# The transform of the long filters: as one full product, and as two half-size products that pass through DRAM

## The chip, the cores and the metric

The kernel runs on one core of one Trainium2 chip. The metric is the time of one execution on the device, in microseconds. A core has a matrix engine (TensorE; the profile calls its matmuls PE and its weight loads PEld), three engines for elementwise work (VectorE = DVE, ScalarE = ACT, GpSimd = POOL) and a queue engine (SyncE = SP). Each engine runs its own list of instructions in order and waits on semaphores for the others. Data reach on-chip memory by DMA; matmuls write into eight banks of PSUM.

## The reference, cut to what matters

One encoder layer on 512 tokens of width 2048. Half of its mixing branch is a Hyena operator: a gated long convolution whose filter is itself computed by a small network (33 to 64 to 64 to 64 to 2048 = 1024 channels forward and 1024 backward).

```python
h = jnp.sin(fr * (z @ w1 + b1))            # three layers of this kind, 64 wide
...
h = h @ w4                                 # last layer: 2 x 1024 channels
h_fwd = h[:, :HYENA_W] * decay
h_bwd = h[:, HYENA_W:] * decay
k = jnp.concatenate([h_fwd, jnp.zeros((1, HYENA_W), f32), h_bwd[:0:-1]], axis=0)
k = k / jnp.sum(jnp.abs(k), axis=0, keepdims=True)
...
z = hv * x1
z = bidir_fft_conv(z, filt) + hy_bias * z  # circular convolution of length 2L = 1024
y_h = z * x0
```

Beside it run grouped-query attention, gates, an output projection and a SwiGLU feed-forward layer; they are not changed.

## The kernel before

All matrices are kept transposed (channels on the 128 rows, 512 tokens along a row). A float32 product is made of three float32r products: each operand is split into a high part (a cast on ScalarE) and a low part (a subtraction on VectorE), and `mm3` issues high x high, high x low and low x high. Weights come as tiles of eight 128x128 blocks: `wblk` (L165 to L167) loads a tile on SyncE's queue (`wr`), casts it on ScalarE (`wh`) and subtracts on VectorE (`wl`), with three tiles of each part alive; 24 matmuls use up one tile.

The main line of the first stage is `group`: 16 blocks of three matmuls for one output tile (`px`, `phv`), for the three projections of each of eight channel tiles. After each block it calls `step()`, which advances a queue of generators by one step; a `yield n` in a generator lets n blocks of the main line pass. So the side work of the Hyena branch is sewn into the projections, and its place in TensorE's list is fixed by these counts (`mm` keeps program order). The other engines' lists are put in order by the scheduler of the build.

The side work is, in this order: `mlp_gen` (the three Sin layers; products `hp`, result `h`), then for each of four slices of 256 channels `filter_gen(q)` and `conv_gen(q)`. `filter_gen` loads `w4`, multiplies it with `h` in float32 (64 rows; products `fp`, L308), multiplies by the decay (`fd`, `bd`, L310), forms sum and difference of the two directions (`hs`, `hd`), transposes them (`ktp`) and splits the four tiles (`ks`). `conv_gen` transposes and splits the data (`ztp`, `zt`), and then for each of four frequency tiles `k` makes the filter's spectrum and the data's spectrum, multiplies them and transforms back:

```python
for j in range(4):
    mm3(kp, Th[j][:, ks], Tl[j][:, ks], ksT[j][0], ksT[j][1], j == 0, j == 3)
K = work(f"K{q}{k}")                       # two ScalarE and two VectorE passes turn kp into K (L372 to L375)
yield 3
up = ps_tile(f"up{q}{k}")                  # 12 matmuls of 256 columns, from zT
...                                        # Y = up * K (L384 to L388), split into Yt
yield 3
if k > 0:
    inverse(k - 1)                         # 12 matmuls of 256 columns into ab
    yield 3
```

`T` are the tables of the 512x512 transform in two parts, loaded once by POOL's queue. `tmp` hands out five rotating scratch tiles, `work` six. At a slice's end `abs` and `y` (L400 to L408) bring the result back to the token order and add the bias term; `y` and `yh` are their tiles.

Of the kernel before, what the change touches and what calls it, by code (L numbers as in the profile page):

```python
# [10 lines left out]
F32 = mybir.dt.float32  # L11
F32R = mybir.dt.float32r
AF = mybir.ActivationFunctionType
ALU = mybir.AluOpType
# [83 lines left out]
    return out  # L98


def layer_kernel(tc, wpk, xT, par, flt, zemb, w4, decT, tbl, rope, qkg, out):
    nc = tc.nc
    PSUM = bass.MemoryType.PSUM

# [44 lines left out]
    def tmp(name):  # L149
        return tpool.tile([P, S], F32, tag="tmp", bufs=5, name=name)  # L150
# [113 lines left out]
    Th, Tl = [], []  # L264

    C1 = 6.28125
    C2 = float(np.float32(2 * math.pi - C1))
# [5 lines left out]
    def mlp_gen():  # L273


        hcur = zem
        yield MLP_WAIT
        for l in range(3):
            nk = 33 if l == 0 else 64
            hp = ps_tile(f"hp{l}")  # L280
            mm(hp[:64], fl[:nk, l * 64:(l + 1) * 64], hcur[:nk], True, True)
            a = tmp(f"ha{l}")[:64]
            nn = tmp(f"hn{l}")[:64]
            nc.vector.tensor_scalar(a, hp[:64], fl[:, 192 + l:193 + l], fl[:, 195:196], ALU.add, ALU.mult)
# [5 lines left out]
            hcur = (tmp(f"h{l}") if l < 2 else cw("h3", [P, S], "h3"))[:64]  # L290
            nc.scalar.activation(hcur, a, AF.Sin)
            yield MLP_WAIT
        mlp["h"] = hcur

    filt = {}

    def filter_gen(q):

        w4s = cw(f"w4{q}", [64, 512], "w4", 1)
        nc.scalar.dma_start(w4s, w4[q])  # L300
        rn, hs_l, hd_l = [], [], []
# [26 lines left out]
        ksT = []  # L328
        for j in range(4):
            tp = ps_tile(f"ktp{q}{j}")  # L330
            for i, src in enumerate((hs_l[0], hs_l[1], hd_l[0], hd_l[1])):
                transpose(tp[:, i * P:(i + 1) * P], src[:, j * P:(j + 1) * P])
            ksT.append(split(cv, tp, "kh", "kl", 4, 4, f"ks{q}{j}"))
            yield 2
        filt[q] = (rn, ksT)

    zst, x0st, yh = {}, {}, [None] * HT

    def conv_gen(q):

        rn, ksT = filt[q]
        while q not in zst or side["n"] < zst[q][2]:
            yield 1
        zl, zf_l, _ = zst[q]
# [20 lines left out]

        for k in range(4):
            ks = slice(k * P, (k + 1) * P)
            kp = ps_tile(f"kp{q}{k}")
            for j in range(4):
                mm3(kp, Th[j][:, ks], Tl[j][:, ks], ksT[j][0], ksT[j][1], j == 0, j == 3)  # L370
            K = work(f"K{q}{k}")
            nc.scalar.activation(K[:, :256], kp[:, :256], AF.Copy, scale=pcol("cosw", k))  # L372
            nc.scalar.activation(K[:, 256:], kp[:, :256], AF.Copy, scale=pcol("nsinw", k))
            nc.vector.scalar_tensor_tensor(K[:, :256], kp[:, 256:], pcol("sinw", k), K[:, :256], ALU.mult, ALU.add)
            nc.vector.scalar_tensor_tensor(K[:, 256:], kp[:, 256:], pcol("cosw", k), K[:, 256:], ALU.mult, ALU.add)  # L375
# [630 lines left out]
def _constants():  # L1006
    f4 = np.float32
    i = np.arange(S)
    t64 = np.cos(np.pi * ((2 * i[:, None] + 1) * (2 * i[None, :] + 1) % 4096) / 2048.0).astype(f4)
    u = t64.view(np.uint32)  # L1010
    hi = (((u.astype(np.uint64) + 0x7FF + ((u >> 12) & 1)) >> 12) << 12).astype(np.uint32).view(f4)
    lo = t64 - hi
    tbl = np.stack([hi, lo]).reshape(2, 4, P, S)
# [17 lines left out]
    for half, pp in ((0, tok // 64), (1, tok % 64)):  # L1031
# [70 lines left out]
```

## Time and profile before

| | |
|---|---|
| median of 3 runs | 2658.74 us (2657.42 to 2659.44) |
| the profiled execution | 2661.56 us |
| its span, first to last instruction | 2659.8 us |
| TensorE busy, share of the span | 99% |
| VectorE, ScalarE, POOL | 61%, 38%, 2% |
| data moved | 293.58 MB, 110 GB/s over the span |
| mean granted TensorE clock | 0.997 of full |

The page's 40 slices show TensorE busy in nine tenths or more of each slice. The filters and the long convolution lie between some 60 and 415 us. The rows on which the prediction rests stand in the section behind the change. In a timeline, a row is the start in us, the duration in us, the engine, the line of the program, the operation, out<-in, and how many instructions of a kind are merged; in brackets is how long the engine was idle ahead of it and who released it. "ACTq" and "POOLq" rows are the issues of DMAs.

### The profile page before, as it was taken

The page shows a single profiled execution, that of the slowest core. Times are in us where ns is not written, and L with a number is a line of the kernel's source. Part 1 is how long each engine was busy: PE and PEld are TensorE (multiplying, and loading weights), DVE is VectorE, ACT ScalarE, POOL GpSimd, SP SyncE. Part 2 cuts the span into 40 slices and gives each one's busy share as a digit, 9 for nine tenths or more (in the row PEclk, how much of TensorE's full clock was granted, in tenths as well). Part 3 has the DMA queues.
Part 4 walks back from the last instruction along what each step waited for, and adds up shares of the span by engine and source line. Part 5 has one row for each costly group of instructions (what it writes and reads, how often), then busy time and mean ns, then how long its engine had stood idle before and what let it go on. Part 6 is the DMA issues. An engine that isn't in the chain of part 4 may idle for free.

```text
span 2659.8 us, 32756 instructions
## 1 busy us (share of the span) xinstructions
PE 2638.1 (99%) x13062; PEld 2219.2 (83%) x13062; DVE 1620.7 (61%) x2285; ACT 1001.2 (38%) x1449; POOL 65.1 (2%) x126
## 2 busy tenths in 40 slices
PE   9999999999999999999999999999999999999999
PEld 7777888788888888888788888888888888788887
DVE  7766654566333333544699898988988862443343
ACT  6333323466222222333454444444444442322111
POOL 0000001110000000000000000000000000000000
PEclk9999999999999999999899999999999999999999
DMA  6222123211223322344333333333333343442343
GB/s 207 78 69 74 60 72 107 80 56 56 96 95 97 101 95 95 123 143 150 99 111 117 121 121 118 127 126 112 121 126 127 118 140 103 153 148 95 123 147 107
DMA packets 90325, 293.58 MB, mean 110 GB/s; under 512 B 10459, under 2 KB 11419, under 8 KB 90172
## 3 DMA queue, kind: packets, MB, share of 16 engines
q1 hardware_dynamic: 71856, 251.69, 29.0%
q10 hardware_dynamic: 12684, 23.02, 2.9%
q0 software_dynamic: 5632, 16.78, 1.6%
q8 instruction: 102, 1.67, 0.3%
q14 instruction: 51, 0.42, 0.0%
HBM read 272.58 MB, written 18.87 MB: 110 GB/s over the span
## 4 chain that ended last, share of the span: by engine, by line
PE 96%; DVE 2%; DMA 1%; ACT 1%; issue 0%; SPq 0%; POOL 0%; ACTq 0%; DVEq 0%; POOLq 0%
PE fx L117 18%; PE d L117 17%; PE g L117 13%; PE fy L117 9%; PE px L117 7%; PE o L117 7%; PE b L117 7%; PE fz L117 5%; PE phv L117 3%; PE q L117 2%; PE kv L117 2%; PE kp L117 2%; PE ab L117 1%; PE up L117 1%; PE av L117 1%; PE sp L117 1%
## 5 line engine op out<-in xcount | busy, mean ns | idle before, releaser
L166 ACT CAST wh<-wr 128x1024 fp32r<-128x1024 f32 (+1 forms) x291 | 304.1, 1046 | 892.7 <-PE d L117 301.0
L167 DVE TENSOR_TENSOR wl<-wr,wh 128x1024 fp32r<-128x1024 f32 (+1 forms) x291 | 352.7, 1212 | 444.8 <-ACT wh L166 442.4
L117 PE MATMUL d<-act,wh 128*128 128x512 f32 x1408 | 435.4, 390 | 2.5 <-DVE act L871 2.0
L117 PEld LDWEIGHTS d<-act,wh 128*128 128x128 f32 x1408 | 264.2, 188 | 60.7 <-DVE act L871 3.9
L781 ACT CAST whs<-s 128x1024 fp32r<-128x1024 f32 x176 | 185.1, 1052 | 244.8 <-PE fx L117 113.1
L117 PE MATMUL d<-act,wl 128*128 128x512 f32 x704 | 273.9, 389 | 0.0
L782 DVE TENSOR_TENSOR wls<-s,whs 128x1024 fp32r<-128x1024 f32 x176 | 214.9, 1221 | 7.6 <-ACT whs L781 2.6
L781 ACT CAST wha<-a 128x1024 fp32r<-128x1024 f32 x132 | 138.9, 1052 | 205.1 <-PE fx L117 97.8
L117 PE MATMUL g<-xh,wh 128*128 128x512 f32 x512 | 200.4, 391 | 0.0
L117 PE MATMUL g<-xl,wh 128*128 128x512 f32 x512 | 199.3, 389 | 0.0
L117 PE MATMUL g<-xh,wl 128*128 128x512 f32 x512 | 199.3, 389 | 0.0
L117 PE MATMUL fx<-X,wha 128*128 128x512 f32 x704 | 179.1, 396 | 5.7 <-DVE c L919 2.9
L117 PE MATMUL fx<-X,whs 128*128 128x512 f32 x704 | 178.1, 395 | 0.4 <-DVE v L797 0.4
L117 PE MATMUL fy<-X,whs 128*128 128x512 f32 x704 | 177.2, 393 | 0.0
L782 DVE TENSOR_TENSOR wla<-a,wha 128x1024 fp32r<-128x1024 f32 x132 | 161.2, 1222 | 8.1 <-ACT wha L781 3.4
L117 PEld LDWEIGHTS d<-act,wl 128*128 128x128 f32 x704 | 132.1, 188 | 27.4
L117 PEld LDWEIGHTS fx<-X,wha 128*128 128x128 f32 x704 | 127.8, 191 | 29.5 <-issue 5.7
L117 PEld LDWEIGHTS fx<-X,whs 128*128 128x128 f32 x704 | 127.6, 190 | 23.9 <-DVE v L797 0.9
L117 PEld LDWEIGHTS fy<-X,whs 128*128 128x128 f32 x704 | 126.8, 189 | 22.7
L117 PEld LDWEIGHTS g<-xh,wl 128*128 128x128 f32 x512 | 96.1, 188 | 20.0
L117 PEld LDWEIGHTS g<-xl,wh 128*128 128x128 f32 x512 | 96.2, 188 | 19.2
L117 PEld LDWEIGHTS g<-xh,wh 128*128 128x128 f32 x512 | 96.2, 188 | 19.1
(1175 smaller groups left out, 4766.8 us busy)
## 6 DMA issues: line engine op xcount, KB each, us to landing
wr<-wpk SPq DMA_DIRECT2D x287, 512.0 KB, 3.3
a<-wpk SPq DMA_DIRECT2D x176, 512.0 KB, 3.8
actd<-c POOLq DMA_DIRECT2D x40, 256.0 KB, 5.0
actr<-actd ACTq DMA_DIRECT2D x40, 256.0 KB, 4.0
xr<-xT SPq DMA_DIRECT2D x16, 256.0 KB, 5.7
x<-xT ACTq DMA_DIRECT2D x16, 256.0 KB, 2.9
x2d<-x POOLq DMA_DIRECT2D x16, 256.0 KB, 3.4
x2r<-x2d ACTq DMA_DIRECT2D x16, 256.0 KB, 2.7
```

Source lines behind the costliest of these rows:

```text
L117: tc.keep_in_program_order(nc.tensor.matmul(out, lhsT=lhsT, rhs=rhs, start=start, stop=stop, **kw))
L166: nc.scalar.copy(hi[:, c], raw[:, c])
L167: nc.vector.tensor_tensor(lo[:, c], raw[:, c], hi[:, c].bitcast(F32), ALU.subtract)
L781: nc.scalar.copy(hi, w)
L782: nc.vector.tensor_tensor(lo, w, hi.bitcast(F32), ALU.subtract)
```

## The change

The filter transform moves from `conv_gen` into `filter_gen` and is done in another way. `hs` and `hd` are stored with their second half reversed, so that rows m and 511-m of the transform meet. After the transposes, each pair of tiles is turned by a position's angle into `u` and `v` (`ku`, `kv`; two ScalarE and two VectorE passes), split, and multiplied by half-size cosine and sine tables `CS` (256 positions by 256 frequencies, loaded by POOL's queue at the start). Sum and difference of the two products (`ke`, `ko`) are the even and the odd frequencies; after the same four passes as before each is written with every second row of a 512x512 DRAM tile `kd[q]`, and `conv_gen` reads it back in frequency order, tile by tile, as `K`. The last layer of the filter network and the one before it change too: the last Sin layer gives its 64 results twice, on 128 rows, and `w4` is held as high part on rows 0 to 63 and low part on rows 64 to 127, so that a product is two float32r matmuls with `hh` and `hl` in place of one float32 matmul.

```diff
-    fl = cw("fl", [64, 196], "fl")
+    fl = cw("fl", [P, 324], "fl")[:, :268]
...
+            nr = 64 if l < 2 else P
-            mm(hp[:64], fl[:nk, l * 64:(l + 1) * 64], hcur[:nk], True, True)
+            mm(hp[:nr], fl[:nk, l * 64:l * 64 + nr], hcur[:nk], True, True)
...
-        mlp["h"] = hcur
+        hh, hl = cw("hh", [P, S], "hh", dt=F32R), cw("hl", [P, S], "hl", dt=F32R)
+        nc.scalar.copy(hh, hcur)
+        nc.vector.tensor_tensor(hl, hcur, hh.bitcast(F32), ALU.subtract)
+        mlp["h"] = hh, hl
...
     def filter_gen(q):
-        w4s = cw(f"w4{q}", [64, 512], "w4", 1)
-        nc.scalar.dma_start(w4s, w4[q])
+        w4r = tmp(f"w4r{q}")
+        w4h = tpool.tile([P, S], F32R, tag="tmp", bufs=5, name=f"w4h{q}")
+        w4s = cw(f"w4s{q}", [P, 512], "w4s", 1, F32R)
+        for h in range(2):
+            nc.scalar.dma_start(w4r[h * 64:(h + 1) * 64], w4[q])
+        nc.scalar.copy(w4h[64:], w4r[64:])
+        nc.scalar.copy(w4s[:64], w4r[:64])
+        nc.vector.tensor_tensor(w4s[64:], w4r[64:], w4h[64:].bitcast(F32), ALU.subtract)
...
-                mm(fp, w4s[:, half * 256 + c * P:half * 256 + (c + 1) * P], mlp["h"], True, True)
+                mm(fp, w4s[:, csl], mlp["h"][0], True, False)
+                mm(fp, w4s[:, csl], mlp["h"][1], False, True)
...
-            nc.vector.tensor_tensor(hs, fd, bd[:, 1:], ALU.add)
-            nc.vector.tensor_tensor(hd[:, ::-1], fd, bd[:, 1:], ALU.subtract)
+            nc.vector.tensor_tensor(hs[:, :256], fd[:, :256], bd[:, 1:257], ALU.add)
+            nc.vector.tensor_tensor(hs[:, :255:-1], fd[:, 256:], bd[:, 257:], ALU.add)
+            nc.vector.tensor_tensor(hd[:, 256:], fd[:, :256], bd[:, 1:257], ALU.subtract)
+            nc.vector.tensor_tensor(hd[:, 255::-1], fd[:, 256:], bd[:, 257:], ALU.subtract)
...
-            ksT.append(split(cv, tp, "kh", "kl", 4, 4, f"ks{q}{j}"))
-            yield 2
+            nc.scalar.activation(u, ab_[0], AF.Copy, scale=fcol("cosb", j))
+            nc.scalar.activation(v, ab_[0], AF.Copy, scale=fcol("nsinb", j))
+            nc.vector.scalar_tensor_tensor(u, ab_[1], fcol("sinb", j), u, ALU.mult, ALU.add)
+            nc.vector.scalar_tensor_tensor(v, ab_[1], fcol("cosb", j), v, ALU.mult, ALU.add)
+            uv.append([split(cv, t, "kh", "kl", 4, 4, f"k{n}{q}{j}") for n, t in (("us", u), ("vs", v))])
+            yield 3
+        yield 6
+        kd[q] = dpool.tile([S, S], F32, tag=f"kd{q}", bufs=1, name=f"kd{q}")
+        for k in range(2):
+            for i in range(2):
+                kp = ps_tile(f"kp{q}{k}{i}")
+                for j in range(2):
+                    sl = slice(j * 256 + k * P, j * 256 + (k + 1) * P)
+                    mm3(kp, CS[i][0][:, sl], CS[i][1][:, sl], uv[j][i][0], uv[j][i][1], j == 0, j == 1)
+                yield 2
+            se = tmp(f"ks{q}{k}")
+            nc.scalar.copy(se, cs[1])
...
+                if i == 0:
+                    nc.gpsimd.dma_start(kd[q][256 * k:256 * k + 255:2], K)
+                elif k == 0:
+                    nc.gpsimd.dma_start(kd[q][1:254:2], K[1:])
+                    nc.gpsimd.dma_start(kd[q][511:512], K[:1])
+                else:
+                    nc.gpsimd.dma_start(kd[q][255:510:2], K)
...
     def conv_gen(q):
         for k in range(4):
-            kp = ps_tile(f"kp{q}{k}")
-            for j in range(4):
-                mm3(kp, Th[j][:, ks], Tl[j][:, ks], ksT[j][0], ksT[j][1], j == 0, j == 3)
             K = work(f"K{q}{k}")
...
-            yield 3
+            nc.gpsimd.dma_start(K, kd[q][ks])
             up = ps_tile(f"up{q}{k}")
...
+    for j in range(2):
+        t = [cw(f"CS{i}{j}", [P, S], f"cs{i}{j}", 1, F32R) for i in range(2)]
+        for i in range(2):
+            nc.gpsimd.dma_start(t[i], tb2[i, j])
+        CS.append(t)
```

The order of instructions changes with it. ScalarE's list around the last Sin layer (`h`), ahead of slice 0's first product, before:

```order
L455 ACTIVATE yh_691<-x00u,prm 128x512
L291 ACTIVATE h_644<-ha_635 64x512
L166 CAST wh_844<-wr_843 128x1024
L315 ACTIVATE scr_766,n_765<-fd_744 128x512
L316 ACTIVATE scr_766,n_765<-bd_745 128x512
L304 DMA dec_777<-decT 128x512
```

and the same place now (`w4r` is the raw tile, `w4s` and `w4h` its parts, `scr` reads the first products' results):

```order
L297 ACTIVATE h_652<-ha_643 128x512
L313 DMA w4r_752<-w 64x512
L519 ACTIVATE yh_699<-x00u,prm 128x512
L301 CAST hh<-h_652 128x512
L313 DMA w4r_752<-w 64x512
L315 CAST w4s_754<-w4r_752 64x512
L166 CAST wh_870<-wr_869 128x1024
L314 CAST w4h_753<-w4r_752 64x512
L333 ACTIVATE scr_786,n_785<-fd_762 128x512
L334 ACTIVATE scr_786,n_785<-bd_763 128x512
```

The load of `w4`, which stood near the start of the program, and its casts now stand between the last Sin and the first passes on the product. VectorE's list at the end of slice 1, ahead of slice 2's first product (`fp`, read by `fd`), before:

```order
L404 SCALAR_TENSOR_TENSOR y_1993<-z_1086,prm,y_1993 128x512
L403 TENSOR_TENSOR y_2000<-abs_1998 128x256
L408 TENSOR_TENSOR yh_1494<-yh_1494,y_1993 128x512
L404 SCALAR_TENSOR_TENSOR y_2000<-z_1380,prm,y_2000 128x512
L310 TENSOR_TENSOR fd_2012<-fp_2014,dec_2010 128x512
L408 TENSOR_TENSOR yh_1650<-yh_1650,y_2000 128x512
```

and now:

```order
L463 SCALAR_TENSOR_TENSOR y_2061<-z_1095,prm,y_2061 128x512
L462 TENSOR_TENSOR y_2068<-abs_2066 128x256
L467 TENSOR_TENSOR yh_1563<-yh_1563,y_2061 128x512
L463 SCALAR_TENSOR_TENSOR y_2068<-z_1427,prm,y_2068 128x512
L316 TENSOR_TENSOR w4s_2078<-w4r_2076,w4h_2077 64x512
L467 TENSOR_TENSOR yh_1695<-yh_1695,y_2068 128x512
L328 TENSOR_TENSOR fd_2086<-fp_2088,dec_2084 128x512
```

The low part of `w4s`, an operand of the product, stands behind the four `y` passes of slice 1. POOL's list behind the loads of the tables `T`, before:

```order
L436 DMA T_415<-tbl 128x512
L436 DMA T_417<-tbl 128x512
L529 TENSOR_TENSOR rpk<-rpk,gaink 128x128 x8
```

and now, the part of slice 0:

```order
L495 DMA T_415<-tbl 128x512
L495 DMA T_417<-tbl 128x512
L395 DMA kd_978<-K_1017 128x512
L397 DMA kd_978<-K_1023 127x512
L398 DMA kd_978<-K_1023 16x1x32
L435 DMA K_1127<-kd_978 128x512
L395 DMA kd_978<-K_1062 128x512
L400 DMA kd_978<-K_1068 128x512
L435 DMA K_1162<-kd_978 128x512
L435 DMA K_1224<-kd_978 128x512
L435 DMA K_1293<-kd_978 128x512
```

Between the tables and the attention's work (`rpk`) now stand nine transfers for each slice; a read waits for the writes of its rows. The four loads of `CS` stand at the very start of POOL's list, the first ahead of the second step of the identity matrix `ident`.

## Rows read from the trace of the kernel before

**Rows 1.** The page, part 1: busy us, share and instructions of each engine.

```profile
PE 2638.1 (99%) x13062; PEld 2219.2 (83%) x13062; DVE 1620.7 (61%) x2285; ACT 1001.2 (38%) x1449; POOL 65.1 (2%) x126
```

**Rows 2.** Busy time by stretch: PE, PEld, DVE, ACT, POOL, clock, DMA share, GB/s.

```profile
60.00:440.00 380.00, 380.00 (x1840) 307.64 (x1840) 230.23 (x397) 121.39 (x184) 3.39 (x8) 1.00 0.23 74
```

**Rows 3.** Timeline of TensorE at the first filter product `kp`, and what follows it.

```profile
104.59 0.39 PE L117 MATMUL kp<-ks00h,T 128*128 128x512 f32 x1
...
107.31 0.39 PE L117 MATMUL phv<-xh,wh 128*128 128x512 f32 x1
```

**Rows 4.** Busy time by stretch, instructions on tile `kp`, then `fp` (without ACT).

```profile
60.00:440.00 380.00, 46.15 (x192) 36.04 (x192) 14.01 (x32) 13.49 (x32) 1.00 0.23 74
...
60.00:440.00 380.00, 17.96 (x32) 4.71 (x32) 10.90 (x16) 1.00 0.23 74
```

**Rows 5.** Timeline of TensorE around the first product `fp` of slice 0.

```profile
76.69 0.39 PE L117 MATMUL px<-xh,wl 128*128 128x512 f32 x1
77.01 1.12 PE L117 MATMUL fp<-h,w 64*128 64x512 f32 x2
78.06 0.50 PE L117 MATMUL px<-xh,wh 128*128 128x512 f32 x1
78.39 0.39 PE L117 MATMUL px<-xl,wh 128*128 128x512 f32 x1
```

**Rows 6.** Timeline of ScalarE around the last Sin layer, `h`.

```profile
72.82 0.82 ACT L455 ACTIVATE yh<-x00u,prm 128x512 f32<-128x512 f32 x1 [1.68 <-DVE x00u L454]
74.89 0.64 ACT L291 ACTIVATE h<-ha 64x512 f32<-64x512 f32 x1 [1.25 <-DVE ha L289]
77.94 1.06 ACT L166 CAST wh<-wr 128x1024 fp32r<-128x1024 f32 x1 [2.42 <-DMA wr<-wpk]
```

**Rows 7.** Timeline of VectorE there: the clamp of `ha`, and a weight split.

```profile
74.45 0.41 DVE L289 TENSOR_SCALAR ha<-ha 64x512 f32<-64x512 f32 x1
...
75.44 1.21 DVE L167 TENSOR_TENSOR wl<-wr,wh 128x1024 fp32r<-128x1024 f32 x1
```

**Rows 8.** Issue to landing: the loads of `w4` (L300), of `T`, the writes of `x2d`.

```profile
DMA to landing us min/median/max: 2.4/2.6/6.4
DMA to landing us min/median/max: 3.1/4.2/5.9
DMA to landing us min/median/max: 2.3/2.9/3.6
```

**Rows 9.** Timeline of TensorE in the feed-forward layer, behind an idle stretch.

```profile
1323.79 3.75 PE L117 MATMUL fx<-X,wha 128*128 128x512 f32 x8 [2.89 <-DVE c L919]
...
1330.21 2.09 PE L117 MATMUL fx<-X,wha 128*128 128x512 f32 x8
```

**Rows 10.** Busy time by stretch at that place, columns as in rows 2.

```profile
1324.00:1326.00 2.00, 2.00 (x5) 1.57 (x6) 2.00 (x3) 0.46 (x1) 0.00 (x0) 0.50 0.00 0
...
1328.00:1330.00 2.00, 2.00 (x12) 2.00 (x12) 0.30 (x1) 1.04 (x2) 0.00 (x0) 0.55 0.02 4
```

**Rows 11.** Timeline of VectorE at the end of slice 1.

```profile
227.85 0.69 DVE L454 TENSOR_TENSOR hv4u<-phv,rbc 128x512 f32<-128x512 f32 x1 [2.79 <-PE phv L117]
...
235.30 0.75 DVE L404 SCALAR_TENSOR_TENSOR y<-z,prm,y 128x512 f32<-128x512 f32 x1
235.97 0.69 DVE L310 TENSOR_TENSOR fd<-fp,dec 128x512 f32<-128x512 f32 x1
```

**Rows 12.** Timeline of TensorE there: the first product of slice 2.

```profile
233.28 1.12 PE L117 MATMUL fp<-h,w 64*128 64x512 f32 x2
```

**Rows 13.** Instructions on tile `kp`: the passes that make `K`; ns min/median/max.

```profile
L372 ACT ACTIVATE K<-kp,prm x16: 476/476/476, 107.5 to 398.9; 128x256 f32<-128x256 f32 x16
...
L374 DVE SCALAR_TENSOR_TENSOR K<-kp,prm,K x16: 478/484/486, 108.4 to 399.7; 128x256 f32<-128x256 f32 x16
```

**Rows 14.** Busy time by stretch at the start, columns as in rows 2.

```profile
5.00:10.00 5.00, 3.29 (x17) 2.37 (x17) 3.04 (x7) 2.94 (x7) 0.00 (x0) 1.00 0.89 289
...
15.00:20.00 5.00, 4.47 (x20) 3.42 (x19) 4.22 (x6) 3.86 (x7) 0.00 (x0) 1.00 1.02 384
```

**Rows 15.** The page, part 3: POOL's DMA queue, packets, MB, share of 16 engines.

```profile
q0 software_dynamic: 5632, 16.78, 1.6%
```

More of the change, by code (lines that the diff above doesn't have):

```diff
@@ L98, in weight_blocks, with layer_kernel @@
     return out
-def layer_kernel(tc, wpk, xT, par, flt, zemb, w4, decT, tbl, rope, qkg, out):
+def layer_kernel(tc, wpk, xT, par, flt, zemb, w4, decT, tbl, tb2, rope, qkg, out):
     nc = tc.nc
@@ L263, in layer_kernel, with fcol @@
     nc.scalar.dma_start(zem[:33], zemb)
-    Th, Tl = [], []
+    Th, Tl, CS = [], [], []
+    def fcol(name, i=0):
+        c = {"cosb": 260, "sinb": 262, "nsinb": 264, "row0": 266}[name] + i
+        return fl[:, c:c + 1]
     C1 = 6.28125
@@ L279, in mlp_gen @@
             nk = 33 if l == 0 else 64
+            nr = 64 if l < 2 else P
             hp = ps_tile(f"hp{l}")
-            mm(hp[:64], fl[:nk, l * 64:(l + 1) * 64], hcur[:nk], True, True)
-            a = tmp(f"ha{l}")[:64]
-            nn = tmp(f"hn{l}")[:64]
-            nc.vector.tensor_scalar(a, hp[:64], fl[:, 192 + l:193 + l], fl[:, 195:196], ALU.add, ALU.mult)
+            mm(hp[:nr], fl[:nk, l * 64:l * 64 + nr], hcur[:nk], True, True)
+            a = tmp(f"ha{l}")[:nr]
+            nn = tmp(f"hn{l}")[:nr]
+            nc.vector.tensor_scalar(a, hp[:nr], fl[:nr, 256 + l:257 + l], fl[:nr, 259:260], ALU.add, ALU.mult)
             nc.vector.tensor_scalar(nn, a, float(np.float32(1 / (2 * math.pi))), MAGIC, ALU.mult, ALU.add)
@@ L289, in mlp_gen @@
             nc.vector.tensor_scalar(a, a, PI32, -PI32, ALU.min, ALU.max)
-            hcur = (tmp(f"h{l}") if l < 2 else cw("h3", [P, S], "h3"))[:64]
+            hcur = tmp(f"h{l}")[:nr]
             nc.scalar.activation(hcur, a, AF.Sin)
             yield MLP_WAIT
-        mlp["h"] = hcur
-    filt = {}
-    def filter_gen(q):
-        w4s = cw(f"w4{q}", [64, 512], "w4", 1)
-        nc.scalar.dma_start(w4s, w4[q])
+        hh, hl = cw("hh", [P, S], "hh", dt=F32R), cw("hl", [P, S], "hl", dt=F32R)
+        nc.scalar.copy(hh, hcur)
+        nc.vector.tensor_tensor(hl, hcur, hh.bitcast(F32), ALU.subtract)
+        mlp["h"] = hh, hl
+    filt, kd = {}, {}
+    def filter_gen(q):
+        w4r = tmp(f"w4r{q}")
[6 more added lines that the diff above has]
+        nc.vector.tensor_tensor(w4s[64:], w4r[64:], w4h[64:].bitcast(F32), ALU.subtract)
         rn, hs_l, hd_l = [], [], []
@@ L308, in filter_gen @@
                 fp = ps_tile(f"fp{q}{c}{half}")
-                mm(fp, w4s[:, half * 256 + c * P:half * 256 + (c + 1) * P], mlp["h"], True, True)
+                csl = slice(half * 256 + c * P, half * 256 + (c + 1) * P)
+                mm(fp, w4s[:, csl], mlp["h"][0], True, False)
+                mm(fp, w4s[:, csl], mlp["h"][1], False, True)
                 nc.vector.tensor_tensor(dst, fp, dec, ALU.mult)
@@ L327, in filter_gen @@
         yield 8
-        ksT = []
-        for j in range(4):
-            tp = ps_tile(f"ktp{q}{j}")
-            for i, src in enumerate((hs_l[0], hs_l[1], hd_l[0], hd_l[1])):
-                transpose(tp[:, i * P:(i + 1) * P], src[:, j * P:(j + 1) * P])
-            ksT.append(split(cv, tp, "kh", "kl", 4, 4, f"ks{q}{j}"))
-            yield 2
-        filt[q] = (rn, ksT)
+        uv = []
+        for j in range(2):
+            ab_ = []
+            for h in range(2):
+                tp = ps_tile(f"ktp{q}{j}{h}")
+                for i, src in enumerate((hs_l[0], hs_l[1], hd_l[0], hd_l[1])):
+                    o = h * 256 + j * P
+                    transpose(tp[:, i * P:(i + 1) * P], src[:, o:o + P])
+                ab_.append(tp)
+            u, v = tmp(f"ku{q}{j}"), tmp(f"kv{q}{j}")
+            nc.scalar.activation(u, ab_[0], AF.Copy, scale=fcol("cosb", j))
[4 more added lines that the diff above has]
+            yield 3
@@ new lines, in filter_gen @@
+        yield 6
+        kd[q] = dpool.tile([S, S], F32, tag=f"kd{q}", bufs=1, name=f"kd{q}")
+        for k in range(2):
+            cs = []
+            for i in range(2):
[3 more added lines that the diff above has]
+                    mm3(kp, CS[i][0][:, sl], CS[i][1][:, sl], uv[j][i][0], uv[j][i][1], j == 0, j == 1)
+                cs.append(kp)
+                yield 2
+            se = tmp(f"ks{q}{k}")
+            nc.scalar.copy(se, cs[1])
+            E, O = tmp(f"ke{q}{k}"), tmp(f"ko{q}{k}")
+            if k == 0:
+                nc.vector.scalar_tensor_tensor(E, se, fcol("row0"), cs[0], ALU.mult, ALU.add)
+                nc.vector.scalar_tensor_tensor(O, cs[0], fcol("row0"), se, ALU.mult, ALU.subtract)
+            else:
+                nc.vector.tensor_tensor(E, cs[0], se, ALU.add)
+                nc.vector.tensor_tensor(O, cs[0], se, ALU.subtract)
+            for i, src in enumerate((E, O)):
+                K = work(f"K{q}{k}{i}")
+                c = 2 * k + i
+                nc.scalar.activation(K[:, :256], src[:, :256], AF.Copy, scale=pcol("cosw", c))
+                nc.scalar.activation(K[:, 256:], src[:, :256], AF.Copy, scale=pcol("nsinw", c))
+                nc.vector.scalar_tensor_tensor(K[:, :256], src[:, 256:], pcol("sinw", c), K[:, :256], ALU.mult, ALU.add)
+                nc.vector.scalar_tensor_tensor(K[:, 256:], src[:, 256:], pcol("cosw", c), K[:, 256:], ALU.mult, ALU.add)
+                if i == 0:
[3 more added lines that the diff above has]
+                    nc.gpsimd.dma_start(kd[q][511:512], K[:1])
+                else:
+                    nc.gpsimd.dma_start(kd[q][255:510:2], K)
@@ L337, in layer_kernel @@
+        filt[q] = rn
     zst, x0st, yh = {}, {}, [None] * HT
     def conv_gen(q):
-        rn, ksT = filt[q]
+        rn = filt[q]
         while q not in zst or side["n"] < zst[q][2]:
@@ L367, in conv_gen @@
             ks = slice(k * P, (k + 1) * P)
-            kp = ps_tile(f"kp{q}{k}")
-            for j in range(4):
-                mm3(kp, Th[j][:, ks], Tl[j][:, ks], ksT[j][0], ksT[j][1], j == 0, j == 3)
             K = work(f"K{q}{k}")
[L372 to L375, printed above, removed]
-            yield 3
+            nc.gpsimd.dma_start(K, kd[q][ks])
             up = ps_tile(f"up{q}{k}")
@@ L437, in layer_kernel @@
             lst.append(t)
+    for j in range(2):
+        t = [cw(f"CS{i}{j}", [P, S], f"cs{i}{j}", 1, F32R) for i in range(2)]
+        for i in range(2):
+            nc.gpsimd.dma_start(t[i], tb2[i, j])
+        CS.append(t)
     rbc = cpool.tile([P, S], F32, tag="bc", bufs=1, name="rbc")
@@ L1009, in _constants, with two_part @@
     t64 = np.cos(np.pi * ((2 * i[:, None] + 1) * (2 * i[None, :] + 1) % 4096) / 2048.0).astype(f4)
[L1010 to L1013, printed above, removed]
+    def two_part(t):
+        u = t.view(np.uint32)
+        hi = (((u.astype(np.uint64) + 0x7FF + ((u >> 12) & 1)) >> 12) << 12).astype(np.uint32).view(f4)
+        return np.stack([hi, t - hi])
+    tbl = two_part(t64).reshape(2, 4, P, S)
+    m, j = i[:256], i[:256]
+    arg = (2 * m[:, None] + 1) * j[None, :] % 1024
+    sarg = (2 * m[:, None] + 1) * np.where(j == 0, 256, j)[None, :] % 1024
+    cs = np.stack([np.cos(np.pi * arg / 512.0), np.sin(np.pi * sarg / 512.0)]).astype(f4)
+    tb2 = two_part(cs).reshape(2, 2, 2, P, 256).transpose(0, 1, 3, 2, 4).reshape(2, 2, P, S)
+    b = np.pi * (2 * m + 1) / 2048.0
+    rot = [t.astype(f4).reshape(2, P).T for t in (np.cos(b), np.sin(b))]
+    order = np.stack([2 * j, np.where(j == 0, 511, 2 * j - 1)]).reshape(2, 2, P).transpose(1, 0, 2).reshape(S)
     w = 2 * np.pi * (i + 0.5) / 1024.0
-    cosw = np.cos(w / 2).astype(f4).reshape(4, P).T
-    sinw = (np.where(i % 2 == 0, 1.0, -1.0) * np.sin(w / 2)).astype(f4).reshape(4, P).T
+    cosw = np.cos(w / 2).astype(f4)[order].reshape(4, P).T
+    sinw = (np.where(i % 2 == 0, 1.0, -1.0) * np.sin(w / 2)).astype(f4)[order].reshape(4, P).T
     pos = np.arange(S, dtype=f4)
@@ L1043, in _arrays @@
     assert all(v.dtype == f4 for v in a.values())
-    tbl, cosw, sinw, zemb, decT, rope = _constants()
+    tbl, tb2, rot, cosw, sinw, zemb, decT, rope = _constants()
     blocks = weight_blocks()
@@ L1072, in _arrays @@
     put("one", np.ones((P, 1), f4))
-    flt = np.zeros((64, 196), f4)
+    flt = np.zeros((P, 268), f4)
+    flt[:, 260:266] = np.concatenate([rot[0], rot[1], -rot[1]], 1)
+    flt[1:, 266] = 1.0
     flt[:33, 0:64] = a["flt_w1"]
-    flt[:, 64:128] = a["flt_w2"]
-    flt[:, 128:192] = a["flt_w3"]
+    flt[:64, 64:128] = a["flt_w2"]
+    flt[:64, 128:192] = flt[:64, 192:256] = a["flt_w3"]
     for j, n in enumerate(("flt_b1", "flt_b2", "flt_b3", "flt_freq")):
-        flt[:, 192 + j] = a[n]
+        flt[:64, 256 + j] = flt[64:, 256 + j] = a[n]
     w4 = a["flt_w4"].reshape(64, 2, NQ, 256).transpose(2, 0, 1, 3).reshape(NQ, 64, 512)
```

4 lines of the change are left out of this document (2 added, 2 removed).

## The prediction

> **What bounds the kernel now.** The first line of the page gives TensorE 2638.1 us of busy time in a span of 2659.8 [rows 1]. A busy matrix engine alone proves little, so I took the stretch that the change touches: from 60 to 440 us TensorE is busy for 380.00 of 380.00 us, VectorE for 230.23, ScalarE for 121.39 [rows 2]. So there the time goes down only if TensorE has less to do, and goes up wherever TensorE is made to wait. Then the timeline of TensorE, for the pace: the twelve matmuls of one filter product (tile `kp`) start 2.72 us before the next projection matmul does, 0.227 us each [rows 3]. I use that pace for every 128x512 matmul, and half of it for 128x256.
>
> **What is removed.** (1) The full transform is sixteen `kp` groups of twelve matmuls, the 192 of [rows 4]. The two half-size products take 4 slices x 2 halves x 2 (cosine, sine) x 2 blocks x 3 = 96 of the same shape. 96 fewer at 0.227 are **-21.8 us**, all on the engine that is never idle here. (2) The last filter layer is 16 float32 products, 32 records in [rows 4], two for each. One of them puts two ordinary matmuls that would start 0.227 us apart 1.70 us apart in sum (76.69 to 78.39, with one ordinary matmul in it) [rows 5]: 1.70 - 0.45 = 1.25 us for one product. Two float32r matmuls with 128 rows take 0.45. 16 x 0.79 = **-12.7 us**. The transposes stay 16 a slice. Sum: -34.5 us.
>
> **What is added beside TensorE.** VectorE gets, for each of four slices, four combinations at 0.75, four more splits' low parts net of the four it had, four E/O sums at 0.69, and a low part of `w4`, some 7 us, 28 in all. ScalarE gets some 20. With 150 us of VectorE idle in [rows 2] this costs nothing as work; it costs where TensorE, which runs its list in order, reaches a product before its operand. So I walked through every place where TensorE now meets a new operand.
>
> **First filter product (slice 0).** Before, its weights were loaded early and nothing is waited for. Now `w4` lands in a scratch tile of the rotating pool, so its two loads stand in ScalarE's list behind the last Sin, and the operand needs a chain: load, two casts on ScalarE with a weight tile's cast between them, that weight tile's low part on VectorE, then the low part of `w4s`. Before, Sin starts at 74.89 and TensorE takes the product at 77.01 [rows 5, 6]. In VectorE's list a weight split of 1.21 us that stood behind the clamp now stands ahead of it [rows 7], and one pass of 0.6 moved behind it, so Sin starts near 75.5. Then: `yh` 0.82 and the cast `hh` 0.6, to 77.0; the second half's load issues there and lands 2.6 later (the median of the four loads of `w4`) [rows 8], 79.6; its cast to 80.3; the weight tile's low part to about 80.8 and the 64-row subtract 0.6: 81.4. TensorE has nothing else in its list: **+4.5 us**, 4 with quicker loads, 8 with the slowest landing of [rows 8], 6.4.
>
> **The clock.** The trace shows what such a gap costs afterwards. At 1323.79 TensorE starts again after 2.89 us idle, the granted clock is 0.50 of full (1.2 of 2.4 GHz), and eight matmuls take 3.75 us that take 2.09 at full clock [rows 9, 10]. That stretch runs to about 1329; at half clock it loses 2.6. I add **+3 us** to each gap of over 2.5 us.
>
> **First product of slice 2.** The same loads come behind the previous slice's end. The trace of before shows that chain: `hv4u` starts at 227.85, the last `y` at 235.30 and ends 0.67 later [rows 11]; the new low part of `w4s` stands right behind it in VectorE's list, 0.6: 236.6. TensorE is there at 233.28 [rows 12]. **+3.4 us**, and 3 for the clock; 2.5 to 5 for the gap. In slices 1 and 3 the low part stands some twenty matmuls earlier against TensorE's list, so there it is covered.
>
> **Data spectrum (`up`).** The `kp` products stood between the transposed data and `up` and hid its split. Now 6 matmuls, 1.4 us, are left for a cast of about 0.6 and a subtract of 0.69. Slice 0 has other work ahead of both on their engines: **+1 us**, 0 to 2.
>
> **The way through DRAM.** After the second half product of `k`=0, `K` needs a copy, E and O (0.69 each) and four passes of 0.48 on either engine, overlapped [rows 13]: 4.9 us. Then three writes, landing 2.3 to 3.6 after issue, and a read, 3.1 to 5.9 [rows 8]: there 10.8 to 15 us after that product. TensorE comes to `inverse(0)`, which needs Y of it, some 18 us after the product by its list (51 ordinary matmuls, two half products, two `up` groups at half the pace, 17.0, and eight transposes), less 3.6 for Y and its split: 14.4. So it just fits; **0**, up to 2 in all. The second quarter has 9 us more and fits. POOL's waits hold up nobody else: behind them in its list stand the rotary tables, after the last slice.
>
> **The start.** The four new tables (1 MB) are issued by POOL at once, ahead of the second step of `ident`, into a stage in which the DMA is 0.89 to 1.02 busy at 289 to 384 GB/s and TensorE idles [rows 14]. 1 MB at 384 GB/s is 2.7 us, part of it into gaps: **+1.5 us**, 0 to 5 (if a gap there also drops the clock).
>
> **Sum.** -34.5 + 4.5 + 3.4 + 6 + 1 + 1.5 = -18.1 us. The profiled execution took 2661.56 us, the span and 1.8 around it: 2643.5. The median of the runs shown is 2658.74, 2.8 lower, and runs are what will be compared: **2641 us**.
>
> **Rivals.** (B) The waits are covered: ScalarE and VectorE run ahead of the order I took, the loads of `w4` land while TensorE is still on other work. For: 150 us of slack on VectorE. Against: each chain is in-order and its start hangs on TensorE itself. -34.5 + 1.5 to 3: 2626 us. (C) The other side: the DRAM trip ends last. The write of the odd rows of `k`=0 has 127 rows, a shape that no row shows on this queue. POOL's queue kept its engines busy for 1.6% of 16 x 2659.8 us, 681 us, for 16.78 MB [rows 15], 24.6 GB/s for one engine. If the 127 rows go through one engine alone, 260 KB take 10.6 us, not 0.7, and `K` lands 9.9 later, at 20.7 to 25 against 14.4. It turns against the kernel from a delay of about 4 us for each slice on: then a gap of 6 to 10 us, and 3 for the clock, come three times (slices 0 to 2; slice 3 has over 100 matmuls in between), 27 to 39 us: -18.1 + 33 = +15, **2674 us**. The Trainium skill, page "DMA: Bandwidth & Descriptors", section "Why a DMA increments its semaphore by 16 and not by 1", says that a copy is spread over the largest number up to 16 that divides its outer dimension, so 127 rows go to one engine; it also tells of an exception, that POOL's queue gave some direct copies all sixteen, 127 rows among them. By the rule it would be C, by the exception the sum above; no run here shows it yet. I hold the spread for likelier, since the transfers of this queue in the trace are all such direct copies. (D) The half-finished case: only one of the two gaps turns out as large as worked out, or the start costs its 5 us: 2632 to 2652, inside the range.
>
> **How the numbers follow.** Forecast with D, 0.62; B, 0.16; C, 0.22. The range has to take in B and the upper ends of the forecast's own terms (-34.5 + 8 + 5 + 6 + 2 + 2 + 5 = -6.5: 2652), and leaves C out but for a mild one, whose gap is just past the point from which it decides: 2624 to 2662. A measurement of this kernel tells about 0.2%, 5.3 us, from no change; below 2653.4 is faster. Faster: nearly all of the forecast and B, 0.75. Same: the forecast's upper tail and the lower edge of C, 0.07. Slower: the rest of C, 0.18.
>
> **What would show it.** In the profile after: 96 `kp` records, at 0.227 us; 32 records of `fp` at the ordinary pace; on TensorE a wait of 4 to 5 us at `fp` of slice 0 and one of 3 to 4 at slice 2, both put down to VectorE (`w4s`), with a granted clock near 0.5 for some 6 us behind each; no wait over 1 us at `ab`. Waits at `ab` in slices 0 to 2 that trace back to `Y`, `K` and a late DMA on POOL's queue would be C. No waits at `fp` would be B. The forecast is wrong as a whole if the stretch to the end of the filters is not shorter by 15 to 20 us while everything behind it keeps its length.

## The result, and the profile after

The changed kernel takes 2643.11 us (median of 6 runs, 2642.02 to 2646.29) beside 2658.84 us of the kernel before: a ratio of 0.9938, 95% interval 0.9927 to 0.9949. That is 15.7 us less; the forecast was 2641 us. The profiled execution took 2646.29 us with a span of 2644.5, 15.3 below that of before; it is the slowest of the six, probably for the two-valued times of the last section.

The page of the changed kernel, part 1 (answers to [rows 1]) and POOL's queue in part 3 (answers to [rows 15]):

```profile
PE 2610.4 (99%) x12966; PEld 2208.5 (84%) x12966; DVE 1643.9 (62%) x2338; ACT 1020.7 (39%) x1482; POOL 86.5 (3%) x166
...
q0 software_dynamic: 8896, 26.22, 2.8%
```

TensorE's busy time fell by 27.7 us, but the span by 15.3. So there is idle time that was not there. The same stretch as [rows 2 and 4], first all instructions (PE, PEld, DVE, ACT, POOL), then those on tile `kp`, then those on `fp` (without ACT); clock, DMA share and GB/s stand at the end:

```profile
60.00:440.00 380.00, 368.26 (x1824) 309.74 (x1823) 266.70 (x485) 151.27 (x251) 27.03 (x52) 0.99 0.32 102
...
60.00:440.00 380.00, 24.91 (x96) 18.01 (x96) 10.86 (x16) 4.69 (x8) 0.99 0.32 102
...
60.00:440.00 380.00, 11.47 (x32) 6.62 (x32) 10.69 (x16) 0.99 0.32 102
```

96 `kp` and 32 `fp` records, as read from the diff. TensorE, never idle here before, is now idle for 11.74 of 380 us. What it waits for, from its list of waits (line waited for, us in all, times, longest), with the three rows that lie in this stretch:

```profile
PE fp L117 <- DVE w4s L316: 10.1, 2, 6.6
...
PE up L117 <- DVE zt01l L189: 1.1, 1, 1.1
...
PE ktp L120 <- DVE hd L345: 0.5, 1, 0.5
```

10.1 + 1.1 + 0.5 is all of it. No row names `ab`: the way through DRAM makes TensorE wait nowhere. The timeline of TensorE at the two places of `fp`, slice 0 and slice 2:

```profile
76.84 0.39 PE L117 MATMUL px<-xh,wl 128*128 128x512 f32 x1
83.88 0.76 PE L117 MATMUL fp<-hh,w4s 128*128 128x512 f32 x1 [6.64 <-DVE w4s L316]
84.44 0.63 PE L117 MATMUL fp<-hl,w4s 128*128 128x512 f32 x1
...
231.13 0.50 PE L117 MATMUL fp<-hh,w4s 128*128 128x512 f32 x1 [3.47 <-DVE w4s L316]
231.47 0.39 PE L117 MATMUL fp<-hl,w4s 128*128 128x512 f32 x1
```

Busy time by stretch behind the two waits, columns as above; the third value from the end is the granted clock:

```profile
84.00:86.00 2.00, 2.00 (x5) 1.61 (x6) 0.69 (x1) 0.17 (x1) 0.00 (x0) 0.50 0.76 260
...
90.00:92.00 2.00, 2.00 (x11) 1.62 (x10) 1.08 (x8) 0.34 (x2) 0.00 (x0) 1.00 0.50 131
232.00:234.00 2.00, 2.00 (x7) 1.52 (x6) 0.59 (x1) 1.00 (x3) 0.00 (x0) 0.52 0.00 0
```

A clock of 0.50 is 1.2 of 2.4 GHz. From 83.88 on, 13 matmuls take 5.31 us that take 2.95 at the pace of [rows 3]; from 231.13 on, 13 take 4.67. That is 2.4 + 1.7 = 4.1 us more.

Why slice 0 waits 6.6 us and not 4.5, in ScalarE's timeline and then VectorE's:

```profile
75.53 0.63 ACT L297 ACTIVATE h<-ha 128x512 f32<-128x512 f32 x1 [4.23 <-DVE ha L295]
75.54 0.53 ACTq L313 DMA_DIRECT2D w4r<-w  x1
...
76.23 0.48 ACTq L313 DMA_DIRECT2D w4r<-w  x1
76.94 0.60 ACT L301 CAST hh<-h 128x512 fp32r<-128x512 f32 x1
80.19 0.62 ACT L315 CAST w4s<-w4r 64x512 fp32r<-64x512 f32 x1 [2.64 <-DMA w4r<-w]
80.71 1.04 ACT L166 CAST wh<-wr 128x1024 fp32r<-128x1024 f32 x1
81.78 0.61 ACT L314 CAST w4h<-w4r 64x512 fp32r<-64x512 f32 x1
```

```profile
81.78 1.23 DVE L167 TENSOR_TENSOR wl<-wr,wh 128x1024 fp32r<-128x1024 f32 x1 [2.70 <-ACT wh L166]
83.04 0.69 DVE L316 TENSOR_TENSOR w4s<-w4r,w4h 64x512 fp32r<-64x512 f32 x1
```

The first load takes 4.6 us from issue to landing instead of the 2.6 of the forecast. ScalarE stands at the cast that needs it, so the weight tile's cast (`wh`), whose own load landed at 76.69, does not run in its shadow but behind it, and VectorE's 1.23 us for that weight tile then stands ahead of the low part of `w4s`.

At slice 2 VectorE comes to the low part right behind the last `y` pass of slice 1, and TensorE starts when it is done:

```profile
229.61 0.74 DVE L463 SCALAR_TENSOR_TENSOR y<-z,prm,y 128x512 f32<-128x512 f32 x1
230.38 0.69 DVE L316 TENSOR_TENSOR w4s<-w4r,w4h 64x512 fp32r<-64x512 f32 x1
```

### The profile page after: what moved, and what is told of

Same layout as the page of the kernel before. It is cut to its first block, busy times and chain, and to the rows that moved or that the text cites. A ratio compares the mean times of both kernels' runs of the same rounds, so it can differ in the third digit from the quotient of the medians.

```text
span 2644.5 us, 32721 instructions
## 1 busy us (share of the span) xinstructions
PE 2610.4 (99%) x12966; PEld 2208.5 (84%) x12966; DVE 1643.9 (62%) x2338; ACT 1020.7 (39%) x1482; POOL 86.5 (3%) x166
## 4 chain that ended last, share of the span: by engine, by line
PE 94%; DVE 3%; DMA 1%; ACT 1%; issue 1%; ACTq 0%; DVEq 0%
PE fx L117 19%; PE d L117 18%; PE g L117 13%; PE fy L117 9%; PE o L117 7%; PE b L117 7%; PE px L117 6%; PE fz L117 5%; PE phv L117 3%; PE q L117 2%; PE kv L117 2%; PE up L117 1%; PE kp L117 1%; PE ab L117 1%; PE av L117 1%; PE sp L117 1%
```

## The experiments

Theory 1 is the forecast's: what TensorE no longer has to do is gone in full, and 14 us of it come back, nearly all through the one late operand `w4s`. The rivals: the waits belong to the half-size transform; the way through DRAM is at its limit; something else is late as soon as `w4s` is not. For comparing profiles I use, beside the medians, the time from the third filter layer's matmul (`hp`, the start of its row) to the last `kv` matmul, read from TensorE's timeline: 382.1 us before, 364.6 after. It holds the whole change but its start.

**The half-size transform alone.** The last filter layer as before, the rest as changed:

```
-        w4r = tmp(f"w4r{q}")
...
-        nc.vector.tensor_tensor(w4s[64:], w4r[64:], w4h[64:].bitcast(F32), ALU.subtract)
+        w4s = cw(f"w4{q}", [64, 512], "w4", 1)
+        nc.scalar.dma_start(w4s, w4[q])
...
-                mm(fp, w4s[:, csl], mlp["h"][0], True, False)
-                mm(fp, w4s[:, csl], mlp["h"][1], False, True)
+                mm(fp, w4s[:, csl], mlp["h"], True, True)
```

> Only the half-size transform; the last filter layer stays as in the kernel before (64 rows, float32, weights loaded early into a buffer of their own). Theory 1 (the waits at fp belong to the layer alone): the half-size products bring -21.3 us, and what they uncover costs 2.8 (1.1 at up, 0.5 at ktp, 1.2 of pace): 2640 us, that is, as fast as the whole change or faster, and no wait at fp. Theory 2 (each part saves what its matmuls say, the waits come from the transform): 2643 + 13 = 2656 us, with the waits of 6.6 and 3.5 us still in the trace.

2640.44 us, ratio 0.9932 (0.9920 to 0.9945): as fast as the whole change. In its list of waits no `fp` stands, and `up` does:

```profile
PE up L117 <- DVE zt01l L189: 1.1, 1, 1.1
```

From `hp` to the last `kv` it takes 362.2 us; less the wait of 1.1 that is 21.1 below before, against the 21.8 of the forecast.

**The layer alone.** The same lines the other way, in the kernel before, with its last layer `hp2` on 128 rows:

```
-        w4s = cw(f"w4{q}", [64, 512], "w4", 1)
-        nc.scalar.dma_start(w4s, w4[q])
+        w4r = tmp(f"w4r{q}")
...
+                mm(fp, w4s[:, csl], mlp["h"][0], True, False)
+                mm(fp, w4s[:, csl], mlp["h"][1], False, True)
```

> Only the last filter layer on 128 rows; the transform stays full size. Theory 1: -13 us of matmuls, +10.1 us of waits at fp of slices 0 and 2, +4.1 us of half clock behind them: within 3 us of before, 2656 to 2662. Theory 2 (the waits come with the half-size transform): 2646 us and no wait at fp.

2662.63 us, ratio 1.0010 (1.0001 to 1.0018): no gain, if anything a small loss. The waits come with it:

```profile
PE fp L117 <- DVE w4s L311: 10.7, 3, 7.0
```

So the waits belong to the layer, and what the layer saves on TensorE it gives back. In the whole change it is worth nothing: 2643.1 with it, 2640.4 without.

**More work ahead of the product.** One line in the changed kernel:

```
          nc.vector.tensor_tensor(w4s[64:], w4r[64:], w4h[64:].bitcast(F32), ALU.subtract)
+         yield 14
```

> The changed kernel with 14 more steps (42 matmuls, 9.5 us) between the preparation of w4s and the first filter product of each slice. Theory 1 (the two waits and the clock behind them are all that the chain of w4s costs, and nothing else is late next): 2643 - 14 = 2629 us, 2627 to 2633; no wait over 1 us at fp, clock 1.00 there. Theory 2 (the late operand only moves the wait: the later filter meets the DRAM trip or the end of the slice): waits of some 5 us at kp, ab or in the stretch behind the filters, 2637 us or more.

2631.87 us, ratio 0.9897 (0.9883 to 0.9910). Both waits at `fp` are gone, and the granted clock is 1.00 over 60 to 440 us. The expected 2629 lies 2.9 lower; part of what came back is a row of smaller waits, 3.3 us in this stretch against 1.6 (1.1 + 0.5) without the edit, the largest at `up`:

```profile
PE up L117 <- DVE zt01l L189: 0.9, 1, 0.9
PE up L117 <- DVE zt10l L189: 0.8, 1, 0.8
PE up L117 <- DVE zt11l L189: 0.6, 1, 0.6
```

**The operand earlier instead.** Loads and split of `w4` in functions of their own, called for slice 0 ahead of the second and third filter layer, for the others behind the previous slice's `fp` products; the order of TensorE's list is unchanged.

```
+            if l == 1:
+                w4_load(0)
+            if l == 2:
+                w4_split(0)
             hp = ps_tile(f"hp{l}")
...
+        if q + 1 < NQ:
+            w4_load(q + 1)
         yield 8
+        if q + 1 < NQ:
+            w4_split(q + 1)
```

> The changed kernel with the loads and the split of w4 issued earlier (slice 0: one filter layer earlier; the others: in the slice before). The order of TensorE is that of the changed kernel. Theory 1 (in slice 0 another chain is late next: the split of the filter's hidden layer now stands behind a weight cast that waits for its load): slice 2's wait and its clock go (-5.2), slice 0's shrinks to some 3 us: 2634 us. Theory 2 (w4 alone is the cause): no wait over 1 us at fp, 2629 us.

2634.13 us, ratio 0.9902 (0.9887 to 0.9918), as theory 1 said. Slice 2 waits no more; slice 0 waits for the next chain, the split of the hidden layer, 2.2 and 0.5 us. ScalarE's timeline shows what stands in its way: a weight cast, which follows `h` at once and waits for no load, and `yh`:

```profile
78.00 0.64 ACT L316 ACTIVATE h<-ha 128x512 f32<-128x512 f32 x1 [5.24 <-DVE ha L314]
78.54 1.03 ACT L166 CAST wh<-wr 128x1024 fp32r<-128x1024 f32 x1
79.47 0.81 ACT L535 ACTIVATE yh<-x00u,prm 128x512 f32<-128x512 f32 x1
80.19 0.60 ACT L320 CAST hh<-h 128x512 fp32r<-128x512 f32 x1
```

**The loads alone earlier.** POOL issues them, behind the loads of `T`, and no longer ScalarE behind the last Sin:

```
-            nc.scalar.dma_start(w4r[h * 64:(h + 1) * 64], w4[q])
+            nc.gpsimd.dma_start(w4r[h * 64:(h + 1) * 64], w4[q])
```

> The changed kernel with the two loads of w4 issued from POOL's queue, ahead of the last Sin, instead of behind it in ScalarE's list. Theory 1 (of slice 0's wait of 6.6 us some 3 are the late loads, which took 4.6 us beside a weight load and held the weight's cast up; the rest is the order of the lists: a weight cast of 1.05 and a weight low part of 1.22 stand ahead): the wait shrinks to 3.7 us, slice 2's 3.5 stays, 2640 us. Theory 2 (the order of the lists alone): 6.6 us as before, 2643. Theory 3 (the loads alone): the wait goes, 2635 us.

The wait of slice 0 is 3.9 us (3.7 was expected), slice 2's stays:

```profile
PE fp L117 <- DVE w4s L316: 7.4, 2, 3.9
```

So the late loads cost some 2.8 of the 6.6 us, and the 3.9 that are left are the order of the lists: ScalarE and VectorE wait for no load there. The parting is not exact, since ScalarE's list moved a little with the edit (the weight cast now stands ahead of both casts of `w4`). The median, 2643.98 us (2639.26 to 2644.68), doesn't show the gain; from `hp` to the last `kv` the profile does, 361.2 against 364.6. Its start is 1.7 us longer (`hp` at 61.94 against 60.23), for a reason that the last experiment shows.

**A longer way through DRAM.** Ahead of each load of `K`, one copy more from DRAM to DRAM, then two:

```
+         src = kd[q][ks]
+         for t in range(n):
+             hop = dpool.tile([P, S], F32, tag=f"hop{q}{k}{t}", bufs=1, name=f"hop{q}{k}{t}")
+             nc.gpsimd.dma_start(hop, src)
+             src = hop
-         nc.gpsimd.dma_start(K, kd[q][ks])
+         nc.gpsimd.dma_start(K, src)
```

> The changed kernel with the filter spectrum copied once more from DRAM to DRAM ahead of its load: 3.3 us more on the way of each quarter. In the trace after, the first quarter is in SBUF by about 123.7, 196.2 and 270.2 us, is taken at 127.4, 197.7 and 272.6, and the operand made from it is ready 1.1, 1.8 and 1.0 us ahead of ab: 3.4 to 4.9 us to spare. Theory 1 (that is the cover): no wait over 1 us at ab, 2643 to 2645 us. Theory 2 (the way through DRAM is at its limit already): waits of 2 to 3 us at ab in slices 0 to 2, 2652 us or more.

2646.86 us, ratio 0.9953 (0.9938 to 0.9967): between the theories, nearer to the first. It costs 3.7 us by the medians. In its profile TensorE waits 3.2 us longer than in the profile after, 2.2 of them once, in slice 1 at the second `ab`. There the quarter is taken late:

```profile
210.11 0.69 DVE L448 TENSOR_TENSOR Y<-up,K 128x512 f32<-128x512 f32 x1 [5.54 <-DMA K<-hop]
...
213.80 0.51 PE L117 MATMUL ab<-T,Yt11h 128*128 128x256 f32 x2 [2.17 <-ACT Yt11h L188]
```

My account had looked at the first quarter of each slice alone. In the changed kernel VectorE already waits 1.6 us for the second quarter of slice 1, unseen by TensorE; that was the thinnest cover.

> The same with two more copies, 6.6 us. Theory 1 (3.4 to 4.9 us to spare): waits at ab of some 2, 3.5 and 3.5 us in slices 0 to 2, and half clock behind them, 2650 to 2662 us. Theory 2 (the cover is longer, since the lists move with it): under 2646 us. Theory 3 (it was at its limit): 2665 us or more.

2660.49 us, ratio 1.0003 (0.9992 to 1.0013). The three waits that theory 1 put at 2, 3.5 and 3.5 us in slices 0 to 2 are there, at 1.6, 3.1 and 4.5; its list of waits shows the longest first:

```profile
PE ab L117 <- ACT Yt20h L188: 4.5, 1, 4.5
PE ab L117 <- ACT Yt10h L188: 3.1, 1, 3.1
...
PE ab L117 <- ACT Yt00h L188: 1.6, 1, 1.6
```

So 6.6 us more on this way cost the whole gain, 3.3 us a quarter of it.

**Cover for the data's split as well.** On the kernel with 14 steps:

```
              zT.append(split(cv, tp, "zh", "zl", 2, 2, f"zt{q}{j}"))
-             yield 2
+             yield 2 if j == 0 else 4
```

> The kernel with 14 more steps ahead of the first filter product (2631.9 us), and two more steps (6 matmuls, 1.4 us) between the transposed data and the first up product of each slice. Theory 1 (the waits of 0.9, 0.8, 0.6 and 0.3 us at up come from the split of the data, which the full transform used to hide): they go, 2629.5 us. Theory 2 (they only move to ab): 2632 us, with as much wait at ab.

2626.32 us, ratio 0.9877 (0.9862 to 0.9891), 16.8 us below the changed kernel. From `hp` to the last `kv` TensorE is idle for 1.0 us; what is left of its waits there:

```profile
PE ab L117 <- ACT Yt00h L188: 0.8, 1, 0.8
...
PE ab L117 <- DVE Yt00l L189: 0.2, 1, 0.2
```

This is the fastest version found, and it gives the clean size of what was removed: 349.6 - 1.0 against 382.1 is 33.5 us, the forecast's first term being 34.5.

**The start.** The `CS` loads held back by a one-column write from the sum of squares, once on the kernel of 2626 us, once on the changed kernel:

```
+         nc.scalar.copy(t[i][:, :1], acc1[:, :1])
          nc.gpsimd.dma_start(t[i], tb2[i, j])
```

> The kernel of 2626.3 us with the four CS loads held back until the sum of squares of x (a one-column write from it stands ahead of each), some 50 us into the program instead of at its start. In the profiles so far the third filter layer's matmul hp starts at 60.13 and 59.24 us without these loads at the start, and at 60.2 to 61.9 (mean 61.1 of eight) with them. Theory 1 (they cost the start 1.4 us): hp at 59.2 to 60.2, 2625 us. Theory 2 (they cost nothing, the spread is that of the start): hp anywhere up to 61.9, 2626 us.

> The changed kernel with the same edit of the CS loads alone. Theory 1: hp at 59.2 to 60.2, 2641.7 us. Theory 2: hp up to 61.9, 2643 us. In both the waits at fp stay at 6.6 and 3.5 us.

`hp` starts at 59.74 and 59.20 us, as theory 1 said; with before and the layer alone that is four profiles without these loads at the start, mean 59.6, against eight with them, mean 61.1. The medians, 2628.88 (ratio 0.9883, 0.9868 to 0.9898) and 2640.78 us (0.9932, 0.9915 to 0.9948), go up by 2.6 in one case and down by 2.3 in the other: 1.5 us is below what they tell. The rows tell it, the times don't.

The eight are of two kinds. In each of them TensorE waits 1.2 to 2.7 us some 11 us into the program; in four (the half-size transform alone is one) the granted clock then falls and `hp` starts at 61.7 to 61.9 us, in the other four, the changed kernel's among them, it stays at full and `hp` starts at 60.2 to 60.6. Busy time by stretch in these two:

```profile
13.00:15.00 2.00, 2.00 (x6) 1.51 (x6) 0.61 (x1) 0.88 (x1) 0.00 (x0) 0.50 1.04 325
...
13.00:15.00 2.00, 2.00 (x11) 1.65 (x10) 0.71 (x2) 1.37 (x2) 0.00 (x0) 1.00 1.05 386
```

The four at full clock start 0.9 us later on average than the four without these loads at the start; the rest of the 1.5 is half clock, which four of the eight have and four have not.

## Why the prediction was right

**What is removed: right.** -34.5 forecast, 33.5 measured. The transform gave 21.1 of 21.8; what is left for the layer is about 12.4 of 12.7. Taking one pace from a row of the unbroken stretch and counting matmuls was good to 3%.

**First product of slice 0: right place, right cause, too small.** 4.5 forecast, 6.6 measured, inside the bounds of 4 to 8. Two steps of the chain were off. I took the median of `w4` in [rows 8] for the landing; here the first load, issued 0.35 us behind a weight tile's of 512 KB, took 4.6. But I also counted from the second half's issue, at 77.0, while the cast needs only the first half, issued at 75.54; so the landing came 0.6 later than forecast, 80.16 against 79.6. The larger miss is the order: I let the weight tile's cast and low part pass in the load's shadow, though in ScalarE's list that cast stands behind the one that waits for the load. It makes most of the other 1.7 us by which `w4s` is late (83.7 against 81.4). The fifth experiment asks another question, what the wait is when no load is late: 3.9.

**First product of slice 2: right.** 3.4 forecast, 3.5 measured, behind the `y` passes as [rows 11] had it and the rows of the profile after show it.

**The clock: right in kind, smaller.** 6 forecast for two gaps, 4.1 measured. The price came from the feed-forward layer's gap [rows 9], where half clock lasted longer ([rows 10], with 0.55 over 1328 to 1330 us, put its end nearer to 1330 than to the 1329 of the prediction, and the loss nearer to the 3 that I added than to 2.6). It is no fixed price either: over the forty matmuls behind each wait the same two waits lose 4.2 us in the profile after, 4.8 with one copy more and 3.2 with the `CS` loads held back, where the second of them loses 0.2.

**`up`: right.** 1 forecast, 1.1 measured, in slice 0 alone. The wait of 0.5 at `ktp` in slice 1 was not foreseen: VectorE's passes for the sum and difference of the two directions (`hs`, `hd`, each now in two halves) end just too late there.

**The way through DRAM: right.** No wait at `ab`. The rival C fell on its first premise: the write of 127 rows lands in 2.6 to 2.7 us, beside 2.3 to 3.7 for those of 128 rows (minimum, median, maximum of L397, then L395):

```profile
DMA to landing us min/median/max: 2.6/2.7/2.7
...
DMA to landing us min/median/max: 2.3/2.7/3.7
```

That is the exception in the Trainium skill, page "DMA: Bandwidth & Descriptors", section "Why a DMA increments its semaphore by 16 and not by 1", and not its rule. But C had the turning point right: it was put at about 4 us of delay, and with 3.3 more the kernel keeps 12 us of its gain, with 6.6 none. My own account of the cover was thinner than it should have been, since it followed the first quarter of slice 0 and wrote "the second quarter has 9 us more"; in slice 1 the second quarter was the late one.

**The start: right on the mean.** 1.5 forecast; in the one profile after it seemed to be 0.1 (`hp` at 60.23 against 60.13), over twelve profiles 1.5. The two kinds among the eight are what its upper end allowed for, a gap there that also drops the clock.

**Rival B**, that the waits are covered, didn't come by itself, but it is what the third and eighth experiments make: 2626.3 us, the 2626 of its sum.

In the profiled execution the terms add up to -33.5 + 6.6 + 3.5 + 4.1 + 1.1 + 0.5 = -17.7 for the stretch, where 17.5 were measured (382.1 to 364.6). The end came only 15.3 earlier. Most of the missing 2.2 us, 1.6 of them at one place, come behind the last `kv` and are not of the change, as the next but one section shows. That the sum came within some 2 us of the median is in part luck: the 2.1 us too little at slice 0 and the 1.9 too much for the clock cancel.

## What to carry to other kernels

Where one engine never idles, work taken off it is worth its row's pace to a few per cent, and the whole risk is in the operands: for every new operand write down the last instruction that makes it, what stands ahead of it in that engine's list, and how much of the bound engine's list lies between the maker's start and the use. A saving of 12 us was lost entirely because its operand's five-step preparation was begun at the point of use; one `yield` that put 9.5 us of other matmuls in between brought most of it back (2631.9 us against 2640.4 without the layer). And time a combined change in its parts: here one half did all the work.

## What the runs showed of the hardware that I had not expected

A wait of 2.1 us on TensorE costs half clock in some executions and none in others. Each of the twelve profiles has the same wait ahead of the attention, at `qT00p`, for VectorE's `q0o`. In the changed kernel and then in the kernel with 14 steps, TensorE's timeline and the busy time by stretch right behind it:

```profile
487.03 0.33 PE L120 MATMUL qT00p<-ident,q0o 128*128 128x128 f32 x1 [2.07 <-DVE q0o L627]
...
488.57 0.63 PE L117 MATMUL q<-wh,xl 128*128 128x512 f32 x1
```

```profile
488.00:490.00 2.00, 2.00 (x9) 1.63 (x8) 0.70 (x2) 0.26 (x1) 0.00 (x0) 0.52 0.80 264
```

```profile
475.71 0.33 PE L120 MATMUL qT00p<-ident,q0o 128*128 128x128 f32 x1 [2.08 <-DVE q0o L628]
...
477.04 0.39 PE L117 MATMUL q<-wh,xl 128*128 128x512 f32 x1
```

```profile
476.70:478.70 2.00, 2.00 (x13) 1.65 (x12) 0.69 (x2) 0.30 (x1) 0.00 (x0) 1.00 0.88 266
```

From the last `kv` to the first `sp` matmul it is 69.3 us in five profiles (before among them) and 70.9 in seven (after among them), with nothing between. From the first `fx` to the first `d` of the feed-forward layer, where two waits of 2.3 and 2.9 us lie, it is 872.7 to 873.1 us in seven profiles and 875.6 to 876.1 in five. Nothing in the changed code touches either place. So an execution of this kernel carries up to some 4.6 us of such two-valued time at these two places, the profile after happened to have both, and much of the spread of the runs may be this. What decides it I have not settled: neither the length of the wait (2.07 to 2.10 us on both sides) nor whether there were waits earlier in the kernel parts the two groups, since the half-size transform alone has no wait over 1.2 us between 60 us and there and is among the seven, and the changed kernel with the `CS` loads held back has the waits of 6.5 and 3.5 us and is among the five.

Nor is it only short waits. In that last kernel slice 2's wait at `fp` is the 3.47 us of the profile after, but the granted clock behind it is 1.00, where 0.52 stands in the section on the result:

```profile
230.63 0.50 PE L117 MATMUL fp<-hh,w4s 128*128 128x512 f32 x1 [3.47 <-DVE w4s L316]
```

```profile
232.00:234.00 2.00, 2.00 (x11) 1.62 (x10) 0.84 (x3) 1.66 (x3) 0.00 (x0) 1.00 0.00 0
```

13 matmuls take 3.12 us from 230.63 on, and took 4.67 there. The Trainium skill, page "TensorE: Matmul & The Clock Gate", section "Part 1: The HAM clock gate (the "warmup" mystery)", says that the gate's view of activity runs free of the kernel, by which chance would decide; no run here can show that.
